# Encoder layer on one core: bias tables built during the first feed-forward, a place for the first value weights, stacks loaded as halves on two queues

## The chip, the cores and the metric

The kernel runs on one core of one Trainium2 chip. A core has a matrix engine (TensorE, PE in the profile; its weight loads are PEld), a vector engine (VectorE, DVE), a scalar engine (ScalarE, ACT), GpSimd (POOL) and a sync engine (SyncE, SP). Here SP and POOL issue nearly all DMAs, that is transfers between the device's memory (DRAM) and the on-chip memory (SBUF). PE writes its results to accumulator banks (PSUM). Each engine works through its own list of instructions in order; a wait of one instruction holds up those behind it on that engine.

The metric is the device time of one execution in microseconds (us). Lower is better.

## The reference, cut to what matters

One layer of a bidirectional encoder, with 1024 tokens of 1024 features, in float32:

```python
h = swiglu(rmsnorm(x, ffn1_pre_g), w_gate, w_up, w_down)      # d_ff = 2816
x = x + 0.5 * rmsnorm(h, ffn1_post_g)
qkv = rmsnorm(x, mix_pre_g) @ w_qkv                           # 16 heads of 64
o_na  = neighbourhood_attention(q[:8], k[:8], v[:8], rel_bias)
o_dil = dilated_mixture_attention(q[8:], k[8:], v[8:], t5_bias)
x = x + rmsnorm(concat(rmsnorm(o_na), rmsnorm(o_dil)) @ w_out, mix_post_g)
x = x + 0.5 * rmsnorm(swiglu(rmsnorm(x, ffn2_pre_g), ...), ffn2_post_g)
```

Neighbourhood (NA) heads attend, on a grid of 16 rows of 64 tokens, to 8 rows by 16 columns around a token, with a learned bias for each head and each offset in rows and columns; what lies outside is masked. Dilated heads mix three windows (128 tokens with step 1, 512 with step 4, 2048 with step 16) under a T5 bias that depends on the distance alone; the three results are weighted by their softmax denominators.

## The kernel before

**Arithmetic.** Each large product in float32 is three matmuls: both operands are split into a high and a low part (`hi`, `lo`: a cast on ACT, then a subtraction on DVE), and hi·hi, hi·lo and lo·hi are summed in a bank (lines 251, 252, 253, called from many places). The large products of the feed-forwards and of q, k and v are made in blocks by a scheme of seven half-size products in place of eight, so sums of operand blocks are made first, and the partial results are kept and combined.

**Stages, by their place in the trace.**

- 0 to 460 us: gate and up products of the first feed-forward, in 22 blocks (`PairGemm`, `NF` = 22). The first nine blocks have two of their seven products done ahead, while the operand is still being made. The rest part runs from about 93 to 460 us with one turn for each block.
- 460 to 683: the down projection (`Passes`: seven passes over the weights, numbered 0 to 6, each with its own weights `pw`, split at lines 602 and 603).
- 683 to 826: the values. Passes 0 and 1 come first (`vp.run(0, 1)`, 683 to 710), then the first products of the query and key blocks (`pg.ahead`, 710 to 765; weights `whi`, `wlo`, lines 344 and 345), then the values' other passes (765 to 826).
- 826 to 938: the rest of the queries and keys, which are written to DRAM (`qk`).
- 938 to 1062: eight dilated heads, two to a pair (`DilPair`). 1062 to 1200: eight NA heads of eight units each (`na_head`, units of 128 queries).
- 1200 to 1350: output projection and norms. 1350 to 1954: the second feed-forward.

**Bias tables.** `build_bias` runs once, during the values. From the T5 bias it makes two tables by a small matmul (`tabp`, line 755), and writes each to DRAM (`tab`) and from there with one DMA of 2 MB (`gab<-tab`, line 760) as 8 heads × 128 shifted rows, so that a head's bias is a plain load later. For the NA heads it fills `nb` in DRAM (8 × 128 × 384) with the mask value (`neg`, line 763), then copies the learned bias into the places that hold it (16 DMAs `nb<-stk`, line 768). All these DMAs are POOL's.

**Attention.** For each head `load_stack` loads the queries and the two halves of the keys (`st`, 128 × 3 × 1024, 1.5 MB) with four DMAs on POOL's queue, two for each half of 64 partitions. The pool `stk` has two places, and `next_head` loads one head ahead. A dilated head needs its bias `g` (two loads on SP, `g<-gab`) and its queries reordered by residue (a copy on POOL, `q`, line 838); an NA head needs `nb` (one load on SP), to which POOL adds the mask (`L1470`, constant `cmask`) for the units at the inside. A unit is: scores (`sp`, lines 933 and 1037), bias, row maximum and exponential on DVE and ACT (lines 849, 851), transposition of the probabilities on PE (`ptp`, line 859) with a copy to SBUF (`pt`, line 861), and the product with the values (`po`, lines 953 and 1053). PE issues scores three units ahead of the transposition and four ahead of the product.

After the second head of a dilated pair `regroup` brings the results of the windows with a step (`ob`) back to token order with 16 DMAs on SP (line 971); `merge` weights them. `na_v` loads a pair's values with 16 DMAs on SP (line 1011).

**Work between the NA units.** When the dilated heads are done, `attended` puts steps on a list (`c.todo`) of which `c.tick()` takes one, four times in an NA head: sums of squares for the norm on ACT (line 1083), scalings on DVE (line 1090), and "puts" (transposition and split of 128 tokens). Then 32 fillers are set up: three matmuls each of the output projection (`accp`, lines 251 to 253), set between the units at the rate `c.rate`; four make one result in the single bank of the pool `psm`, which ACT copies out (line 291).

**What sets the order.** PE's order is the order of the code, and in the first steps and in the attention that of DVE and ACT also. SP and POOL, and DVE and ACT elsewhere, are ordered by a scheduler from the dependencies. `c.behind(f, engines)` gives `f`'s instructions a place after the last instruction so far of those engines; `plan(n, at)` lays steps on the todo list by turn.

## Time and profile before

| | us |
|---|---|
| median of 3 runs | 1958.9 (1957.07 to 1959.87) |
| the profiled execution | 1956.22 |
| its span | 1954.4 |
| TensorE busy | 1867.5 (96% of the span) |
| DVE busy | 1328.8 (68%) |
| ACT busy | 807.7 (41%) |
| POOL busy | 323.8 (17%) |
| data moved by DMA | 398.63 MB, on average 204 GB/s |

A row of the waits reads "engine tile line <- releaser: us in total, times, longest us". The granted clock is the share of full speed that TensorE was given; where it is below 1, the same matmuls take longer. The DMA share is how busy the core's 16 DMA engines were on average. Durations come from the one profiled execution, not from the median of the runs.

### The profile page before, as it was taken

The numbers are of one execution on the slowest core, as the hardware profiler recorded it, in microseconds if no ns is written. First come the engines' busy times: TensorE is split into PE (matmuls) and PEld (weight loads), VectorE is DVE, ScalarE is ACT, GpSimd is POOL, SyncE is SP. The second block draws the span as 40 slices with busy tenths as digits, with TensorE's granted clock in tenths as the row PEclk, the third lists the DMA queues.
The fourth block names the chain that finished last, engine by engine and source line by source line (L and its number), as shares of the span: only waits on it lengthen the run. The fifth ranks groups of instructions, "written<-read, shape, count | busy, mean of one in ns | idle before, by whom it ended". The sixth has DMA issues, their size and how long they took to land.

```text
span 1954.4 us, 25575 instructions
## 1 busy us (share of the span) xinstructions
PE 1867.5 (96%) x9044; PEld 1557.4 (80%) x9044; DVE 1328.8 (68%) x2235; ACT 807.7 (41%) x1463; POOL 323.8 (17%) x520
## 2 busy tenths in 40 slices
PE   5999999999999999999999788998999999999997
PEld 4788888888888778778898777877888888888886
DVE  5778776765656785567576565676788777755567
ACT  4522233333534454133676555454222333345333
POOL 2101111111000123323444220021011111110000
PEclk8999999999999999999999899999999999999999
DMA  6645565546876667868998982475556665476663
GB/s 244 214 169 178 178 236 195 209 165 252 306 255 206 237 242 263 245 195 246 208 190 158 160 147 47 137 264 205 172 177 203 232 229 185 160 255 226 203 226 140
DMA packets 170433, 398.63 MB, mean 204 GB/s; under 512 B 20080, under 2 KB 41504, under 8 KB 170304
## 3 DMA queue, kind: packets, MB, share of 16 engines
q1 hardware_dynamic: 118800, 222.34, 36.2%
q0 software_dynamic: 50640, 172.55, 28.0%
q10 hardware_dynamic: 864, 2.10, 0.3%
q8 instruction: 71, 1.16, 0.3%
q14 instruction: 58, 0.48, 0.1%
HBM read 272.55 MB, written 127.26 MB: 205 GB/s over the span
## 4 chain that ended last, share of the span: by engine, by line
PE 76%; DVE 7%; DMA 7%; issue 5%; ACT 2%; POOL 2%; SPq 1%; DVEq 0%; POOLq 0%; ACTq 0%
PE mmp L253 15%; PE mmp L251 15%; PE mmp L252 14%; PE accp L251 8%; PE accp L252 8%; PE accp L253 8%; PE po L953 2%; DMA wraw<-in_wqk_dram 2%; PE ptp L859 2%; PE trp L159 1%; PE po L1053 1%; DMA st<-qk 1%; PE sp L933 1%; DMA qk<-qk 1%; DVE wlo L345 1%
## 5 line engine op out<-in xcount | busy, mean ns | idle before, releaser
L251 PE MATMUL mmp<-x,whi 128*128 128x512 f32 (+1 forms) x1464 | 581.1, 397 | 8.2 <-ACT whi L344 3.5
L253 PE MATMUL mmp<-x,wlo 128*128 128x512 f32 (+1 forms) x1464 | 576.4, 394 | 1.1 <-DVE wlo L345 1.1
L252 PE MATMUL mmp<-x,whi 128*128 128x512 f32 (+1 forms) x1464 | 575.8, 393 | 0.6 <-DVE x L161 0.5
L251 PEld LDWEIGHTS mmp<-x,whi 128*128 128x128 f32 x1464 | 278.6, 190 | 68.9 <-ACT whi L344 4.2
L253 PEld LDWEIGHTS mmp<-x,wlo 128*128 128x128 f32 x1464 | 278.5, 190 | 62.4 <-DVE wlo L345 1.9
L252 PEld LDWEIGHTS mmp<-x,whi 128*128 128x128 f32 x1464 | 278.8, 190 | 59.7 <-DVE x L161 1.5
L603 DVE TENSOR_TENSOR pw<-praw,pw 128x1024 fp32r<-128x1024 f32 (+1 forms) x182 | 199.2, 1139 | 121.8 <-ACT pw L602 121.6
L602 ACT CAST pw<-praw 128x1024 fp32r<-128x1024 f32 (+1 forms) x182 | 169.0, 982 | 205.6 <-PE accp L253 163.3
L344 ACT CAST whi<-wraw 128x1024 fp32r<-128x1024 f32 x129 | 135.2, 1050 | 249.0 <-PE mmp L252 227.4
L251 PE MATMUL accp<-pw 128*128 128x512 f32 x600 | 234.5, 391 | 0.0
L253 PE MATMUL accp<-pw 128*128 128x512 f32 x600 | 233.8, 390 | 0.0
L252 PE MATMUL accp<-pw 128*128 128x512 f32 x600 | 233.7, 390 | 0.0
L345 DVE TENSOR_TENSOR wlo<-wraw,whi 128x1024 fp32r<-128x1024 f32 x129 | 157.6, 1224 | 24.0 <-ACT whi L344 23.7
L253 PEld LDWEIGHTS accp<-pw 128*128 128x128 f32 x600 | 112.7, 188 | 23.7
L251 PEld LDWEIGHTS accp<-pw 128*128 128x128 f32 x600 | 112.7, 188 | 23.1
L252 PEld LDWEIGHTS accp<-pw 128*128 128x128 f32 x600 | 112.8, 188 | 22.9
L549 POOL DMA_DIRECT2D g<-sg x44 | 23.8, 541 | 473.3 <-DVE sg L542 286.0
L505 DVE TENSOR_TENSOR c<-mmp,u 128x512 f32<-128x512 f32 x52 | 35.9, 691 | 82.9 <-PE mmp L253 82.6
L363 ACT COPY s<-mmp 128x512 f32<-128x512 f32 x52 | 30.5, 586 | 148.8 <-PE mmp L253 147.2
L344 ACT CAST whi<-traw 128x512 fp32r<-128x512 f32 x52 | 32.3, 621 | 117.5 <-DVE traw L433 58.8
L161 DVE TENSOR_TENSOR x<-trp,x 128x512 fp32r<-128x512 f32 x84 | 57.2, 688 | 34.7 <-ACT x L160 34.7
L432 DVE TENSOR_TENSOR wraw<-wraw 128x1024 f32<-128x1024 f32 x52 | 63.6, 1224 | 23.1 <-DMA wraw<-in_wqk_dram 13.5
(229 smaller groups left out, 2781.5 us busy)
## 6 DMA issues: line engine op xcount, KB each, us to landing
praw<-g SPq DMA_DIRECT2D x70, 512.0 KB
wraw<-in_wg_dram SPq DMA_DIRECT2D x44, 512.0 KB
wraw<-in_wu_dram SPq DMA_DIRECT2D x44, 512.0 KB
tr<-in_wd_dram SPq DMA_DIRECT2D x44, 512.0 KB
g<-sg POOLq DMA_DIRECT2D x88, 256.0 KB, 3.7
ts<-tr POOLq DMA_DIRECT2D x22, 1024.0 KB, 4.7
praw<-ts SPq DMA_DIRECT2D x88, 256.0 KB
praw<-in_wd_dram SPq DMA_DIRECT2D x66, 256.0 KB
```

The costliest lines, as they stand in the source:

```text
L161: nc.vector.tensor_sub(lo, ps, hi.bitcast(F32))
L251: nc.tensor.matmul(out, ahi, bhi, start=start, stop=False, skip_group_check=go_on)
L252: nc.tensor.matmul(out, ahi, blo, start=False, stop=False, skip_group_check=go_on)
L253: nc.tensor.matmul(out, alo, bhi, start=False, stop=stop, skip_group_check=go_on)
L344: nc.scalar.copy(hi, raw)
L345: nc.vector.tensor_sub(lo, raw, hi.bitcast(F32))
L432: nc.vector.tensor_sub(r[:, 0:2], r[:, 1:3], r[:, 0:2])
L505: nc.vector.tensor_add(c21, d, u2)
L602: nc.scalar.copy(hi, raw[:, :m])
L603: nc.vector.tensor_sub(lo, raw[:, :m], hi.bitcast(F32))
L859: nc.tensor.transpose(ps[:, j, :], src[:, j * P:(j + 1) * P], c.ident)
L953: nc.tensor.matmul(po[:, un * 2 + j], pt[:, 2 * j + t, :], rhs, start=t == 0, stop=t == 1)
```

## The change

Five things are changed together.

1. **Tables in steps.** `build_bias` becomes `bias_steps`, which gives small steps to 21 of the 22 turns of the first feed-forward's rest part: the copies of the learned bias in turns 1 to 4, loads and the two table matmuls in turns 2 to 5, the shifted rows two heads at a time in turns 4 to 9, clearing in 6 and 7, filling in 8 to 11. In turns 13 to 21 a masked copy of each NA head's table is made (load, addition on POOL, store to the new `nm` in DRAM). Each step goes behind POOL's last instruction. An NA head now loads both `nb` and `nm`, and POOL's addition in the attention is gone.
2. **First value weights.** A pool `p0` of one place holds the split weights of the values' first group, which are fetched before the last steps of the norm are planned; the plan is 12 turns long in place of 8, with the start of the query and key weights at turn 9 and their first split at 11, into the same pool. The pool `pr` has two places in place of three, and the early weights two and `p0`. The first pass always has its first group cut in two.
3. **Stacks.** Of a stack's two halves, one is loaded by POOL's queue and one by SP's. A third place (from the pool `op`) serves every third of the first nine heads, so that a dilated head's stack is loaded two heads ahead.
4. **Regrouping and values.** Eight of the 16 regroupings follow each quad of blocks, where all 16 followed the second; `na_v` has eight DMAs of 16 partitions where it had 16 of eight.
5. **Work between the units.** `attended` now does the first half's squares and scalings, its four puts and the set-up of the fillers, and then the second half's, each with an empty turn between. There are 16 fillers of six matmuls for 32 of three. Two output weights are fetched at the last dilated head.

```diff
-            for k in range(4):
+            for k in (0, 2):
                 def filler(g=g, t=t, k=k, ws=ws, acc=acc):
...
-                    nat_mm(c, acc[0], x, t, k, ws, True, True)
-                    if k == 3:
+                    for i in (k, k + 1):
+                        nat_mm(c, acc[0], x, t, i, ws, True, True)
+                    if k:
                         c.nc.scalar.copy(part[:, t, g * T:(g + 1) * T], acc[0])
...
     def split_left(self, b):
         if b < self.early:
-            self.w[b] = self.split(self.raw.pop(b), "g")
+            self.w[b] = self.split(self.raw.pop(b), "g", self.own if b % 3 == 0 else None)
             self.fetch_left(b + 2)
...
-        if self.own:
-            self.groups[0] = [groups[0][:2], groups[0][2:]] + groups[1:]
+        self.groups[0] = [groups[0][:2], groups[0][2:]] + groups[1:]
...
-def build_bias(c, rel, t5, onehot, lncount):
+def bias_steps(c, rel, t5, onehot, lncount, cmask):
...
+    def step(turn, f, *args):
+        at.setdefault(turn, []).append(lambda: c.behind(lambda: f(*args), POOL))
...
+    def toeplitz(i, h):
         g = c.gab[i]
-        dst = bass.AP(tensor=g.tensor, offset=g.offset, ap=[[P * 640, 8], [641, P], [1, 511]])
-        nc.gpsimd.dma_start(dst, tab[i, :, :511].unsqueeze(1).broadcast_to([8, P, 511]))
+        dst = bass.AP(tensor=g.tensor, offset=g.offset + h * P * 640, ap=[[P * 640, 2], [641, P], [1, 511]])
+        nc.gpsimd.dma_start(dst, tab[i, h:h + 2, :511].unsqueeze(1).broadcast_to([2, P, 511]))
...
+    def masked(h):
+        if h == 0:
+            got["mask"] = c.bp.tile([P, 384], F32, tag="m", name="mask")
+            nc.gpsimd.dma_start(got["mask"], cmask)
+        if h:
+            t = got.pop(h - 1)
+            nc.gpsimd.tensor_add(t, t, got["mask"])
+            nc.gpsimd.dma_start(c.nm[h - 1], t)
+        if h < 8:
+            got[h] = tile("lc" if h % 2 else "oh", 384)
+            nc.gpsimd.dma_start(got[h], c.nb[h].rearrange("p r e -> p (r e)"))
+    for i in range(2):
+        step(2 + 2 * i, load, i)
+        step(3 + 2 * i, table, i)
+        for h in range(4):
+            step(4 + 2 * i + h, toeplitz, i, 2 * h)
+    for cc in range(8):
+        step(1 + cc // 2, stack, cc)
+    step(6, clear, 0)
+    step(7, clear, 4)
+    for r in range(16):
+        step(8 + r // 4, rows, r)
+    for h in range(9):
+        step(13 + h, masked, h)
...
-def load_stack(c, p, hd):
+def load_stack(c, p, hd, pool, bufs):
...
-    for u in range(2):
-        dst = slice(u * 64, u * 64 + 64)
-        nc.gpsimd.dma_start(st[dst, 0, :], q[u, rows, :])
-        nc.gpsimd.dma_start(st[dst, 1:3, :], k[:, rows, :].rearrange("j p n -> p j n"))
+    for u, queue in enumerate((nc.gpsimd, nc.sync)):
+        to = st[u * 64:u * 64 + 64].bitcast(F32)
+        queue.dma_start(to[:, 0, :], q[u, rows, :])
+        queue.dma_start(to[:, 1:3, :], k[:, rows, :].rearrange("j p n -> p j n"))
...
-        if (hd, part, quad) == (1, 1, 1):
-            self.regroup()
+        if hd and part:
+            self.regroup(quad)
...
-    for r in range(16):
-        c.nc.sync.dma_start(vs[r * 8:r * 8 + 8], src[r])
+    for ci in range(8):
+        c.nc.sync.dma_start(vs[ci:P:8], src[ci])
...
     c.nc.sync.dma_start(nb[:, 0], c.nb[2 * p + hd].rearrange("p r e -> p (r e)"))
+    c.nc.sync.dma_start(nb[:, 1], c.nm[2 * p + hd])
...
-            c.pr, c.pw, c.vt = pool("pr", 3, e), pool("pw", 2, e), pool("vt", 2, e)
+            c.pr, c.pw, c.vt = pool("pr", 2, e), pool("pw", 2, e), pool("vt", 2, e)
...
-            plan(8, {0: [lambda: fin.scale(4, 4), A(4, 5)], 4: [U(4)], 5: [lambda: queued(pg.start)]})
+            p0 = pg.own = pool("p0", 1, prep, side="right")
+            vp.fetch([[p0.tile([P, 2, T], F32R, tag="g" + h, name="pw0" + h) for h in ("hi", "lo")]])
+            plan(12, {0: [lambda: fin.scale(4, 4), A(4, 5)], 8: [U(4)], 9: [lambda: queued(pg.start)],
+                      11: [lambda: pg.split_left(0)]})
...
-            build_bias(c, a["na_rel_bias"], a["t5_rel_bias"], a["onehot"], a["lncount"])
...
-            c.todo.extend([lambda: (queued(c.w.fetch), squares[0]()), squares[1], scales[0],
-                           lambda: (scales[1](), queued(c.w.fetch))]
-                          + puts[:4] + [begin] + puts[4:])
+            c.todo.extend([squares[0], scales[0]] + puts[:4] + [begin, squares[1], lambda: None, scales[1]])
+            for f in puts[4:]:
+                c.todo.extend([lambda: None, f])
...
+            i = next(stacked, None)
+            if i is not None:
+                own = i < 9 and i % 3 == 2
+                stacks.append(load_stack(c, *heads[i], c.op if own else c.stk, 1 if own else 2))
...
-                    else:
-                        nc.gpsimd.tensor_add(g[:, 1], g[:, 0], c.cmask)
...
+                    if (p, hd) == (2 * NP - 1, 1):
+                        queued(lambda: [c.w.fetch() for _ in range(2)])
```

**ACT at the first value weights.** In the list of ACT before, from the last copies of the down projection's stage to the first value copy (`x_…` are operand tiles of the values, `junk,fss` the sums of squares of the norm, `vt` a value result copied out of its bank):

```order
L160 CAST x_4765<-trp 128x4x128
L151 ACTIVATE junk,fss<-hb 128x512
L160 CAST x_4767<-trp 128x4x128
L151 ACTIVATE junk,fss<-hb 128x512 x2
L602 CAST pw<-praw 128x1024
L151 ACTIVATE junk,fss<-hb 128x512
L602 CAST pw<-praw 128x1024
L1362 COPY vt<-accp 128x512
```

After:

```order
L603 CAST pw0hi<-praw 128x1024
L160 CAST x_4858<-trp 128x4x128
L160 CAST x_4860<-trp 128x4x128
L160 CAST x_4858<-trp 128x4x128
L151 ACTIVATE junk,fss<-hb 128x512
L160 CAST x_4860<-trp 128x4x128
L151 ACTIVATE junk,fss<-hb 128x512 x2
L603 CAST pw<-praw 128x1024
L151 ACTIVATE junk,fss<-hb 128x512
L603 CAST pw<-praw 128x1024
L1427 COPY vt<-accp 128x512
L345 CAST whi<-graw 128x1024
```

The first group's cast (`pw0hi`) has moved ahead of the last operand tiles, and the query and key weights' first cast (`whi`) stands right behind the first value copy; before it came some 15 rows later.

**SP from the last dilated heads to the first NA heads**, before (`vs` are an NA pair's values; `g`, `nb` and `obn` as above):

```order
L971 DMA obn<-ob 32x2x132 x16
L895 DMA g<-gab_68 128x384
L895 DMA g<-gab_69 128x384
L1011 DMA vs<-v_87 8x8x128 x17
L1017 DMA nb<-nb 128x384
L971 DMA obn<-ob 32x2x132 x16
L1017 DMA nb<-nb 128x384
L1011 DMA vs<-v_87 8x8x128 x15
```

After:

```order
L1057 DMA vs<-v_87 16x8x128 x8
L1063 DMA nb<-nb 128x384
L1064 DMA nb<-nm 128x384
L106 DMA wraw<-in_wo_dram 128x1024 x2
L1017 DMA obn<-ob 32x2x132 x16
L876 DMA st<-qk_0_73 64x1024
L877 DMA st<-qk_1_74 64x2x1024
L1063 DMA nb<-nb 128x384
L1064 DMA nb<-nm 128x384
L1057 DMA vs<-v_87 16x8x128 x8
```

The last 16 regroupings have moved behind the output weights (`wraw`) and ahead of a stack's half (`st`), which SP did not issue before; each head's `nb` load is followed by one of `nm`.

**PE at the first fillers**, between NA units (`o_…` is the dilated heads' normed result, `accp` the bank of the output projection), before:

```order
L859 MATMUL ptp<-ident,pb 128x128 x3
L251 MATMUL accp<-whi,o_9559 128x512
L252 MATMUL accp<-wlo,o_9559 128x512
L253 MATMUL accp<-whi,o_9559 128x512
L1053 MATMUL po<-vs,pt 128x128 x2
L1037 MATMUL sp<-st 128x384 x2
```

After:

```order
L904 MATMUL ptp<-ident,pb 128x128 x2
L251 MATMUL accp<-whi,o_9591 128x512
L252 MATMUL accp<-wlo,o_9591 128x512
L253 MATMUL accp<-whi,o_9591 128x512
L251 MATMUL accp<-whi,o_9591 128x512
L252 MATMUL accp<-wlo,o_9591 128x512
L253 MATMUL accp<-whi,o_9591 128x512
L1100 MATMUL po<-vs,pt 128x128 x2
L1084 MATMUL sp<-st 128x384 x2
```

Fillers come six matmuls at a time, in every second unit; before, three came in nearly every unit.

More of the change, by code (lines that the diff above doesn't have):

```diff
@@ L592, in fetch @@
             w = c.pr.tile([P, 1 + self.own, 2, 2, T], F32R, tag="w", name="pw")
-            w = [w[:, side] for side in range(1 + self.own)]
+            w = [[w[:, side, h] for h in range(2)] for side in range(1 + self.own)]
         for side in range(1 + self.own):
@@ L600, in fetch @@
                     nc.sync.dma_start(raw[:, j], self.right(i)[b])
-            hi, lo = [w[side][:, h, :m] for h in range(2)]
+            hi, lo = [x[:, :m] for x in w[side]]
             nc.scalar.copy(hi, raw[:, :m])
@@ L604, in fetch @@
         for j, i in enumerate(ids):
[L605 to L606 removed]
+            lhs = [x[:, j, :] for x in w[0]] if self.own else [h[:, i, :] for h in self.left.x[a]]
+            self.ready.append((lhs, [x[:, j, :] for x in w[-1]]))
     def run(self, *which, upto=6):
@@ L1169, in plan @@
             c.todo.extend(turn(at.get(i, ())) for i in range(n))
-        def one_a_turn(steps, n, first):
-            plan(n, {first + i: [f] for i, f in enumerate(steps)})
         def spread(steps, n, skip=0):
@@ L1191, in gate_pairs, with ffn @@
             return PairGemm(c, op, [(wg[f], wu[f]) for f in range(NF)], early, GatePairs(c, which))
-        def ffn(which, op, prep, pg, get, turns, sums, more, post, pre, src, dst, begin=None):
+        def ffn(which, op, prep, pg, get, turns, sums, more, post, pre, src, dst, begin=None, tables={}):
             w = sub()
@@ L1217, in ffn @@
             pg.begin_rest()
-            one_a_turn(sums, NF, NF - 3 - len(sums))
+            tables = {k: list(f) for k, f in tables.items()}
+            if tables:
+                c.bp = pool("bp", 1, w)
+            for i, f in enumerate(sums):
+                tables.setdefault(NF - 3 - len(sums) + i, []).append(f)
+            plan(NF, tables)
             prep2, ps = sub(), []
```

99 lines of the change are left out of this document (54 added, 45 removed).

## The prediction

> **What bounds the kernel now.** I read the page's first two parts first, then busy time by stage, then TensorE's waits in the stages where it isn't full.
>
> ```profile
> PE 1867.5 (96%) x9044; PEld 1557.4 (80%) x9044; DVE 1328.8 (68%) x2235; ACT 807.7 (41%) x1463; POOL 323.8 (17%) x520
> PEclk8999999999999999999999899999999999999999
> ```
>
> TensorE (PE) is busy 96% of the span, so the change, which takes no matmul away, can win only where PE stands still or runs at a lowered clock. The stages (columns: stretch, length, busy us of PE, PE's weight loads, DVE, ACT and POOL, then the granted clock, the DMA share and GB/s):
>
> ```profile
> 60.00:660.00 600.00, 598.94 (x2659) 492.94 (x2658) 427.90 (x539) 223.93 (x305) 65.22 (x115) 1.00 0.62 218
> 660.00:720.00 60.00, 54.66 (x252) 42.87 (x251) 42.16 (x81) 27.43 (x47) 11.88 (x22) 1.00 0.63 223
> 780.00:860.00 80.00, 76.09 (x323) 60.68 (x322) 46.91 (x60) 18.81 (x22) 25.47 (x42) 0.98 0.72 224
> 960.00:1060.00 100.00, 95.50 (x838) 94.39 (x836) 66.40 (x276) 73.18 (x253) 41.03 (x42) 1.00 0.95 176
> 1060.00:1100.00 40.00, 32.74 (x223) 30.35 (x222) 19.45 (x69) 16.88 (x52) 15.46 (x19) 0.87 0.93 161
> 1100.00:1140.00 40.00, 28.90 (x194) 25.78 (x193) 30.07 (x93) 26.08 (x85) 7.24 (x11) 0.91 0.89 153
> 1140.00:1200.00 60.00, 57.40 (x379) 52.00 (x380) 30.80 (x92) 34.48 (x91) 6.50 (x10) 0.97 0.58 110
> ```
>
> The 600 us of the feed-forward are full (598.94 busy). The change touches the other rows, the largest lost shares in 1060 to 1140: idle 7.3 and 11.1 us, and the clock (0.87 and 0.91 of 40 us) loses about 5.2 and 3.6 us more. The DMA engines are nearly full there (0.93, 0.89), the fact that speaks most against a gain.
>
> **A: a place for the first value weights (660 to 720).** PE's waits there:
>
> ```profile
> PE accp L252 <- DVE pw L603: 2.0, 3, 1.0
> PE mmp L251 <- ACT whi L344: 1.7, 1, 1.7
> PE accp L251 <- ACT pw L602: 0.8, 1, 0.8
> ```
>
> They are 4.5 of the 60 − 54.7 = 5.3 us that PE stands: it waits for the first value weights and for the first weights of the queries and keys to be split into high and low parts. Now the first are fetched while the down projection still runs, and the second are split before the values end (pool p0 holds both in turn). I take 4.0 off, because the split merely moves into a stretch where ACT and DVE have room (27.4 and 42.2 of 60). Bounds: 5.3 off, or 1 lost, if the split of QK's weights holds up a value copy behind it on ACT for the longest of these waits less what it saves.
>
> **B: the tables leave the values stage (780 to 860).** PE loses 3.9 us and 2% of clock (1.6). POOL's queue there waits for two tables of 2 MB to land (the last two rows: the landings of all loads and stores of nb, and the tables' issues, with KB and us to landing), at a DMA share of 0.72, against 0.62 in the feed-forward:
>
> ```profile
> POOL nb L768 <- DMA gab<-tab: 16.3, 2, 14.8
> ...
> DVE u L470 <- DMA s<-s1d: 2.9, 1, 2.9
> ...
> PE mmp L251 <- DVE c L497: 2.0, 1, 2.0
> ...
> PE accp L252 <- DVE pw L603: 1.9, 1, 1.9
> ```
>
> ```profile
> DMA to landing us min/median/max: 2.1/4.1/20.2
> ```
>
> ```profile
> gab<-tab POOLq DMA_DIRECT2D x2, 2044.0 KB, 20.5
> ```
>
> DVE made its operand (c) late because the sum s1d, read back from memory, came 2.9 us late. With the two tables, the cleared and the filled bias (1.5 MB each) gone, some 7 MB, such loads come earlier. I take 4.0 off of 5.5; bounds 0 (pr has one place less and this stage's weights may be late anyhow) and 5.5.
>
> **C: the way into the neighbourhood heads (1060 to 1100).** The chain of waits, with columns start, length, what, and PE's waits and SP's queue in the same stretch:
>
> ```profile
> 1063.24 10.28 DMA obn<-ob
> ...
> 1077.51 2.94 DMA nb<-nb
> ...
> 1080.70 0.09 POOL nb L1470
> ...
> 1083.23 11.40 DMA st<-qk
> ...
> 1094.76 0.48 PE sp L1037 x2
> ```
>
> ```profile
> PE po L1053 <- DVE pt L861: 3.2, 1, 3.2
> PE sp L1037 <- DMA st<-qk: 2.1, 1, 2.1
> ```
>
> ```profile
> 1046.61 14.65 SPq L1011 DMA_DIRECT2D vs<-v  x17
> 1061.91 15.49 SPq L971 DMA_DIRECT2D obn<-ob  x16
> ```
>
> Sixteen regroupings (15.5 us of SP) stand ahead of a bias load; POOL's mask addition waits for that load, and the next stack, issued by POOL behind the addition, takes 11.4 us more while PE starves. The change cuts three links: half of the regroupings go out a quad earlier and eight value loads replace 16 (half of 14.65 us), the addition is gone (a masked table is loaded), and a third place lets a stack start one dilated head sooner, some 15 us (eight heads from 938 to 1062). That should remove 3.2 + 2.1 us of waits and 5.2 us of clock; I keep 2 back for the second bias load (1.5 MB in all) and the two output weights (1 MB) that now come in at this point: 8.5 off. Bounds 0 and 10.5.
>
> **D: order of the norm and the fillers (1100 to 1220).**
>
> ```profile
> PE ptp L859 <- DVE pt L861: 4.5, 2, 3.0
> PE po L1053 <- ACT pt L861: 3.0, 1, 3.0
> PE sp L1037 <- DVE stt L849: 1.7, 1, 1.7
> ...
> PE accp L251 <- ACT hs L291: 3.4, 4, 1.0
> ```
>
> ```profile
> L1083 ACT ACTIVATE junk<-og 128x256 bf16<-128x256 f32 x16 | 6.4, 402 | 0.0
> L1083 ACT ACTIVATION_READ_ACCUMULATOR junk<-og 128x1 f32 x16 | 3.0, 189 | 0.0
> L1090 DVE SCALAR_TENSOR_TENSOR og<-og,y,gd 128x512 f32<-128x512 f32 x8 | 6.2, 838 | 0.0
> ```
>
> Here 9.4 us of squares on ACT and 6.2 of scalings on DVE come in lumps between the softmax steps, and the transposed probabilities (pt) queue behind them: 9.2 us of PE waits in the first three rows and 3.6 of clock. After the change one half's squares and scalings are followed by four puts and the first fillers, and the other half comes later, so a lump is half as long and PE has filler matmuls sooner. I take 6 of 12.8: half the waits, and the clock's part with them. Bounds 0 and 11. The fourth row (1140 to 1220) is four waits for the one accumulator bank, each where the next filler stood right behind the last of a bank. Six matmuls in every second unit put a whole unit between: 3.0 off, bounds 1 lost and 3.4.
>
> **E: what is added.** The tables now go to POOL's queue in 21 turns of the feed-forward's 60–460 us, where PE is full and DMA is at 0.62: about 7 MB as before, and 3 MB to read a table, add the mask and write it back, some 10 MB over 360 us or 28 GB/s on 218. Its 8 additions cost POOL, by the next row, 8 × 1.0 to 1.2 us:
>
> ```profile
> L1470 POOL TENSOR_TENSOR nb<-nb,cmask 128x384 f32<-128x384 f32 x3 | 3.6, 1203 | 1.0 <-DVE y L144 1.0
> ```
>
> The work is hidden by POOL's idleness (65 of 600 busy). Behind each waiting table step stand the stores of gate products, which nobody loads before the down projection; if that cover is gone, DVE waits for a place to write, then PE. Two table matmuls stay as they were. SP gets two stack issues and one bias issue more per head, 3 × 0.53 = 1.6 us (the bias load's issue in the queue's rows was 0.35 to 0.53), less the eight value issues. I take 1.7 lost for all of it; bounds 0 and 8 (half of the 16.3 us of POOL waits above, passed on).
>
> **The stacks' halves** go out on two queues. Loads of 64 partitions on POOL's queue, against POOL's loads and stores of all 128 in the feed-forward (200 to 400):
>
> ```profile
> st<-qk POOLq DMA_DIRECT2D x4, 512.0 KB, 8.7
> q0 software_dynamic: 896, 3.15, 47.6%
> ...
> q0 software_dynamic: 5600, 19.93, 25.8%
> ```
>
> A packet took 0.476 × 40 us × 16 / 896 = 340 ns in halves (1140 to 1180) and 147 ns in the feed-forward, at the same 3.5 KB. Half the partitions seem to use about half of what lies on the way; two halves side by side would then land a stack in little over half the time. Of C's 8.5 us I put 3 on this. The Trainium skill disagrees with itself: "DMA: Bandwidth & Descriptors", section "Rules for kernel authors", says of two transfers to disjoint partition halves that they serialize and aren't worth it; "SBUF — State Buffer", section "Door 1: The DMA port swizzle (why `[64,N]` ≈ `[32,N]`)", says that 64 neighbouring partitions reach only half of the 16 ports. No run here shows two halves side by side; the packets favour the second. By the first, the sum would be 3 us smaller.
>
> **Sum.** Among the dilated heads PE waits once for POOL's copy of a late stack, which two heads of lead should end:
>
> ```profile
> PE sp L933 <- POOL q L838: 0.8, 1, 0.8
> ```
>
> −4.0 − 4.0 − 8.5 − 6.0 − 3.0 − 0.8 + 1.7 = −24.6. The profiled execution took 1956.22 us (span 1954.4), 2.7 below the median of 1958.9. So 1931.6 in its terms and 1934 against the median. A change under 0.2% (3.9 us) can't be told from none here.
>
> **Rivals.**
>
> *Attention stays paced by DMA.* For: shares of 0.95, 0.93 and 0.89; the change sends no byte less through these heads, but 1.5 MB more. Against: 0.58 in the last of them, with PE full. Then only A, B and the fillers pay: −4 − 4 − 3 = −11, 1948 us.
>
> *The table steps hold up the feed-forward (slower).* POOL's queue waits there for landings (4.1 us median, 16.3 for the big tables) with gate stores behind each. Passed on in full, 16.3 + 8 × 4.1 = 49 us come to PE; less the 25 won elsewhere, 1983. It decides from the point where the stalls of a turn exceed the stores' slack, and nets zero at 25 us passed on. Against: 535 idle us of POOL in that row.
>
> *SP's queue now waits for a stack's place (slower).* In the neighbourhood heads POOL waits for the place before it issues:
>
> ```profile
> POOL st L831 <- PE sp L1037: 63.3, 5, 16.8
> ```
>
> That is 1090 to 1210; nothing else stood behind it. Now SP waits the same time, with bias and value loads of the next head behind it. If the bias is late by as much as the longest of the PE waits in C, 3.2 us a head over seven heads, that is +22 against the −11 of the first rival: 1970. It decides once a place comes free later than one load before its head begins; the order of SP puts the stack ahead of the same head's bias, which is what speaks for it.
>
> *The halves gain nothing.* Two transfers side by side share what one has: C keeps 3 us, 1937, inside my own range.
>
> **Chances.** My sum 0.60 (0.20 of it with halves that gain nothing), paced by DMA 0.18, tables 0.10, SP's queue 0.12. My sum's own range is 1922 (A to D near their ends, −36) to 1945 (half of C and D missing). For 8 in 10, the low end is 1918 and the high end reaches over the DMA case and the near part of SP's to 1962. Faster is 0.60 + 0.16 of the DMA case; the other 0.02 of it and 0.03 of the two slow cases lie within 0.2%; slower is the remaining 0.19.
>
> **What would show it.** A and B: PE's waits for pw, whi and c gone in those stretches, and the granted clock of B at 1.00. C: no chain through obn, nb and st, no mask addition, a 512 KB half landing nearer 5 than 8.7 us. D: the 4.5 and 3.0 us rows halved, the bank's four waits gone. E: PE still 599 of 600 in the feed-forward; any drop there, or PE waits for bias tiles in the neighbourhood heads, makes me wrong. So does a clock that stays below 0.95 from 1060 to 1140.

## The result and the profile after

The changed kernel takes 1982.7 us (median of four runs, 1980.95 to 1988.07) where the kernel before took 1959.4 beside it: a ratio of 1.0121, with a 95% interval of 1.0107 to 1.0136. It is 23 us slower; 25 us faster were forecast.

The first two parts of the page of the changed kernel (busy time; granted clock in 40 slices):

```profile
PE 1874.5 (95%) x9044; PEld 1562.2 (79%) x9044; DVE 1326.4 (67%) x2235; ACT 808.0 (41%) x1463; POOL 322.4 (16%) x513
PEclk8998898999999999999999989999999999999999
```

PE has the same 9044 matmuls, but the clock now dips in slices 4, 5 and 7, from about 150 to 250 and from 300 to 350 us, where it had been full before. Where the stages begin shows how the time is shared out. By the first matmul of each stage in the two traces:

| from the first matmul of … | before | after | difference |
|---|---|---|---|
| start to the down projection (gate and up products) | 469.0 | 518.8 | +49.8 |
| down projection, first values | 244.0 | 241.2 | −2.8 |
| first products of queries and keys | 52.1 | 51.1 | −1.0 |
| values, rest | 58.7 | 56.7 | −2.0 |
| queries and keys, rest | 114.1 | 109.1 | −5.0 |
| dilated heads | 123.4 | 126.9 | +3.5 |
| NA heads to the second feed-forward | 228.3 | 211.0 | −17.3 |
| second feed-forward, to the last matmul | 653.9 | 655.0 | +1.1 |

Between the gate and up products and the second feed-forward the change wins 24.6 us, close to the 26.3 of the forecast without its last term. The loss is in the first stage, but for 1.1 us of the second feed-forward, which the change doesn't touch. Stretches of the first stage, of the kernel before and then of the changed one (columns as in the prediction):

```profile
160.00:260.00 100.00, 100.00 (x438) 82.11 (x437) 78.82 (x102) 27.97 (x37) 14.17 (x25) 1.00 0.56 197
260.00:420.00 160.00, 160.00 (x698) 131.06 (x697) 115.81 (x140) 55.17 (x76) 21.21 (x36) 1.00 0.59 213
```

```profile
160.00:260.00 100.00, 79.09 (x317) 62.27 (x316) 56.59 (x75) 18.91 (x23) 20.69 (x31) 0.86 0.53 171
260.00:420.00 160.00, 147.59 (x618) 118.48 (x617) 102.72 (x129) 48.19 (x67) 38.45 (x63) 0.96 0.61 210
```

PE stands for 33 of these 260 us; most of the other 17 that the stage lost go with the lowered clock (0.86 and 0.96). The DMA share does not rise; in the worst stretch it even falls, from 0.56 to 0.53, and less is moved (171 for 197 GB/s) although table traffic has been added. Something slow is not something busy. What PE and DVE wait for (changed kernel, 100 to 460 us):

```profile
PE mmp L251 <- DVE c L499: 22.3, 4, 10.9
DVE wraw L434 <- DMA wraw<-in_wu_dram: 15.8, 6, 8.0
...
PE tabp L766 <- DMA oh<-in_onehot_dram: 8.8, 1, 8.8
```

The longest of PE's four waits for DVE, 10.9 us, comes from weights: DVE waits for `wu`, makes its operand (`c`) late, and PE waits for that. (Two others, 6.5 and 4.2 us, come from 308 us on and are taken up under the second rival below.) Once PE itself stands before the table's small matmul. The chain of waits from 160 to 240 us has both:

```profile
168.03 1.12 POOL gab L773
169.15 0.59 POOL tt L759
169.75 16.30 DMA oh<-in_onehot_dram
186.04 0.14 issue
186.18 1.86 PE tabp L766 x2
...
216.17 12.80 DMA wraw<-in_wu_dram
...
232.94 0.61 DVE c L499
233.55 0.04 issue
233.59 0.80 PE mmp L251
```

A load of 64 KB took 16.3 us. It was issued right behind `gab<-tab`, the shifted rows of two heads. The landings in this stretch (160 to 260 us; KB each, median us from issue to landing) name the slow transfer:

```profile
gab<-tab POOLq DMA_DIRECT2D x6, 511.0 KB, 17.0
wraw<-in_wg_dram SPq DMA_DIRECT2D x5, 512.0 KB, 10.0
wraw<-in_wu_dram SPq DMA_DIRECT2D x5, 512.0 KB, 12.7
```

511 KB of shifted rows take 17.0 us. Before the change two DMAs of 2044 KB each, side by side and over eight heads, landed in 20.5: eight times the bytes in hardly more time. In the trace's packet records the first of the new DMAs is 84 packets of 6132 bytes, of which one or two run at once for 13.0 of 13.3 us and never more than three; the two of before have 16 or 17 packets at once for 12.4 of their 20 us, and about eight at their start and end, when one of them runs alone. Packets of 12 bytes stand beside the large ones: 4704 for 672 in the whole changed kernel, which is 14 for each two, and 672 for 672 before, which is eight for each eight; 16 in all both times. At 9 ns each they take little time. The records don't name the engine, but by both counts a DMA with two heads outermost runs on two of the 16 DMA engines, and one with eight heads on eight. A weight load that is spread over all 16 is complete only when its packets on those two are, too. That was the theory with which the experiments began.

The packet records show this wait directly. Two weight loads were issued at 171.4 and 172.0 us and landed at 181.4 and 184.7, while the first rows DMA ran. The mean number of packets in flight:

| stretch of the changed kernel, us | weights | shifted rows | all |
|---|---|---|---|
| 174.0 to 175.5 | 14.5 | 2.0 | 16.6 |
| 176.5 to 185.0 | 0.6 | 1.4 | 2.1 |

Most of the weights' packets were through by 176.5 us. For the 8.5 us behind that about two packets ran at a time, rows and the last of the weights in turn, so most of the 16 engines stood idle. With the tables back in the values (the first experiment below) the same two loads had 16.5 packets in flight at their height and landed after 3.9 and 4.7 us.

### The profile page after: what moved, and what is told of

It reads as the page before. It is cut to its first block, busy times and chain, and to the rows that moved or that the text cites. A ratio compares the mean times of both kernels' runs of the same rounds, so it can differ in the third digit from the quotient of the medians.

```text
span 1980.8 us, 25583 instructions
## 1 busy us (share of the span) xinstructions
PE 1874.5 (95%) x9044; PEld 1562.2 (79%) x9044; DVE 1326.4 (67%) x2235; ACT 808.0 (41%) x1463; POOL 322.4 (16%) x513
## 4 chain that ended last, share of the span: by engine, by line
PE 76%; DMA 11%; DVE 7%; ACT 2%; issue 2%; SPq 1%; POOL 0%; DVEq 0%; ACTq 0%; POOLq 0%
PE mmp L251 15%; PE mmp L252 15%; PE mmp L253 15%; PE accp L252 8%; PE accp L253 8%; PE accp L251 8%; DMA tr<-in_wd_dram 2%; PE po L998 2%; DMA wraw<-in_wu_dram 2%; PE trp L159 2%; PE ptp L904 2%; PE po L1100 1%; PE sp L978 1%; DMA ts<-tr 1%; DMA oh<-in_onehot_dram 1%
## 5 line engine op out<-in xcount | busy, mean ns | idle before, releaser
L251 PE MATMUL mmp<-x,whi 128*128 128x512 f32 (+1 forms) x1464 | 584.9, 400 | 28.4 <-DVE c L499 22.3
```

The source lines that it names most:

```text
L251: nc.tensor.matmul(out, ahi, bhi, start=start, stop=False, skip_group_check=go_on)
```

## The experiments

Each kernel's runs stand beside runs of the kernel before on the same chip. On the chip of experiments 1 to 4 the kernel before took 1963.6 us, on those of 5 to 8 and 9 to 12 it took 1959.6 and 1959.0; a comparison across chips is therefore given by the ratios on 1959 us, and by the medians where these say something else. Times of stages are from one profiled execution of each kernel. "Tables back" below is the first experiment, and several others start from it.

**1. The tables go back.** Only the first part of the change is undone:

```diff
-    bias_steps(c, *[a[k] for k in ("na_rel_bias", "t5_rel_bias", "onehot", "lncount", "cmask")]))
+    )
...
             pg.fetch(1)
+            build_bias(c, a["na_rel_bias"], a["t5_rel_bias"], a["onehot"], a["lncount"])
             vp.run(4, 5)
...
-    c.nc.sync.dma_start(nb[:, 1], c.nm[2 * p + hd])
...
+                    else:
+                        nc.gpsimd.tensor_add(g[:, 1], g[:, 0], c.cmask)
```

> Everything of the change but its first part: the tables are built in one go during the values and the mask is added in the attention, as before. If the table steps alone cost the 50 us that the first feed-forward is longer, the down projection starts near 469 us again and the time is about 1959 - 22 = 1937 us. If the other parts had a hand in it (pools, a longer plan, stacks on SP), it stays above 1960.

Measured 1937.4 us, ratio 0.9856 (0.9828 to 0.9884); the down projection starts at 469.6 us. The table steps cost all of the loss, and the other four parts win 1.4%, as expected.

**2. The tables alone**, put into the kernel before.

```diff
+    bias_steps(c, *[a[k] for k in ("na_rel_bias", "t5_rel_bias", "onehot", "lncount", "cmask")]))
...
-            build_bias(c, a["na_rel_bias"], a["t5_rel_bias"], a["onehot"], a["lncount"])
...
+    c.nc.sync.dma_start(nb[:, 1], c.nm[2 * p + hd])
...
-                    else:
-                        nc.gpsimd.tensor_add(g[:, 1], g[:, 0], c.cmask)
```

> The kernel before with only the first part of the change: table steps in the feed-forward, masked tables loaded in the attention. If the table steps cost 50 us by themselves: 1959 + 50, less some 5 us that the values win without tables, about 2004 us. If they cost only together with the other parts: 1955 to 1965.

Measured 1998.9 us, ratio 1.0182 (1.0159 to 1.0204), that is +36 us by the ratio, where about 45 were expected. The down projection starts at 519.4 us, as in the changed kernel: the 50 us come with the table steps alone. By the medians about 14 come back later. The profile, of the slowest of the four executions (2003.6 us), shows about half of that: 5.2 us in the rest of the queries and keys and 2.3 from the NA heads on, with 4.7 lost again in the dilated heads and the second feed-forward.

**3. Rows outermost.** The same bytes, instructions and places; only the order in which a DMA walks them differs:

```diff
-        dst = bass.AP(tensor=g.tensor, offset=g.offset + h * P * 640, ap=[[P * 640, 2], [641, P], [1, 511]])
-        nc.gpsimd.dma_start(dst, tab[i, h:h + 2, :511].unsqueeze(1).broadcast_to([2, P, 511]))
+        dst = bass.AP(tensor=g.tensor, offset=g.offset + h * P * 640, ap=[[641, P], [P * 640, 2], [1, 511]])
+        nc.gpsimd.dma_start(dst, tab[i, h:h + 2, :511].unsqueeze(0).broadcast_to([P, 2, 511]))
```

> The changed kernel, but each DMA of two heads of shifted rows walks the 128 rows outermost and the heads inside; same bytes, same instructions, same places. Theory 'two engines': as changed, one such DMA runs one or two packets at a time for 13 us, on two of the 16 DMA engines, and every weight load that is spread over all engines waits for those two; with 128 outermost it is spread over all, lands in 4 to 6 us, and most of the stalls from 186 to 260 us go: 1945 to 1960 us. Theory 'order and volume': the steps cost by their place in POOL's queue and their 10 MB, whatever the shape: within 5 us of 1982.

**4. Eight heads in a DMA**, so that eight is the outermost size:

```diff
-        dst = bass.AP(tensor=g.tensor, offset=g.offset + h * P * 640, ap=[[P * 640, 2], [641, P], [1, 511]])
-        nc.gpsimd.dma_start(dst, tab[i, h:h + 2, :511].unsqueeze(1).broadcast_to([2, P, 511]))
+        dst = bass.AP(tensor=g.tensor, offset=g.offset + h * P * 640, ap=[[P * 640, 8], [641, P], [1, 511]])
+        nc.gpsimd.dma_start(dst, tab[i, h:h + 8, :511].unsqueeze(1).broadcast_to([8, P, 511]))
...
-        for h in range(4):
-            step(4 + 2 * i + h, toeplitz, i, 2 * h)
+        step(4 + 2 * i, toeplitz, i, 0)
```

> The changed kernel, but the shifted rows of a table go out as one DMA of 2 MB over eight heads (as before the change), in the turns of the first of the four. 'Two engines': eight engines share what two had, so a stall is shorter but the queue is full for 20 us: between the changed kernel and the one with rows outermost, 1955 to 1975. 'Order and volume': within 5 us of 1982.

Rows outermost: 1946.2 us, ratio 0.9912 (0.9890 to 0.9935). Eight heads: 1965.0, ratio 1.0016 (0.9997 to 1.0034). With two, eight and 128 as the outermost size the kernel is 1.2% slower than before, the same, and 0.9% faster; the down projection starts at 518.8, 496.8 and 481.4 us (469.0 before). Both medians lie in the ranges that were expected under "two engines". Landings from 160 to 260 us with the tables back, with rows outermost, and with eight heads:

```profile
wraw<-in_wg_dram SPq DMA_DIRECT2D x6, 512.0 KB, 4.1
wraw<-in_wu_dram SPq DMA_DIRECT2D x6, 512.0 KB, 5.8
```

```profile
gab<-tab POOLq DMA_DIRECT2D x8, 511.0 KB, 7.3
wraw<-in_wg_dram SPq DMA_DIRECT2D x6, 512.0 KB, 6.6
wraw<-in_wu_dram SPq DMA_DIRECT2D x6, 512.0 KB, 7.7
...
oh<-in_onehot_dram POOLq DMA_DIRECT2D x1, 63.9 KB, 6.0
```

```profile
gab<-tab POOLq DMA_DIRECT2D x2, 2044.0 KB, 17.9
wraw<-in_wg_dram SPq DMA_DIRECT2D x5, 512.0 KB, 6.2
wraw<-in_wu_dram SPq DMA_DIRECT2D x5, 512.0 KB, 8.3
```

The rows land in 7.3 us for 17.0, the weights in 6.6 and 7.7 for 10.0 and 12.7, and the small load in 6.0 for 16.3, so that PE no longer waits at the table's matmul. With eight heads that wait stays, since the load stands behind 2 MB on the same queue (17.6 us to land). That the volume or the place in POOL's queue alone costs the 50 us falls: with rows outermost neither was altered, and 37 of the 50 went. (With eight heads the rows also go out in fewer DMAs and turns, so that step says less by itself.) The Trainium skill states the mechanism in "DMA: Bandwidth & Descriptors", section "Rules for kernel authors": the slowest dimension of a DMA's access pattern sets how many engines it uses, so an outermost size below 16 confines it to at most that many. The landings agree with it, and so do the packets that run at once: one or two with two heads, up to eight for nearly all of the time with eight, up to 16 with 128 rows, where the first copy's large packets are through in 3.5 us and packets of 12 bytes are absent.

Rows outermost still had one stall, of 5.6 us up to 222.8: two DMAs of rows and a clearing of 0.75 MB had been issued from 199.2 to 202.2 us, and the next weight load, issued at 202.5, took 11.0.

**5. Spread steps**: rows outermost, and one DMA of rows in a turn, clearing in four pieces (from a tile of its own), filling earlier and two rows of the grid in a turn.

```diff
...
-            step(4 + 2 * i + h, toeplitz, i, 2 * h)
+            step(4 + 4 * i + h, toeplitz, i, 2 * h)
...
-    step(6, clear, 0)
-    step(7, clear, 4)
+    for h in range(4):
+        step(h, clear, 2 * h)
...
-        step(8 + r // 4, rows, r)
+        step(5 + r // 2, rows, r)
```

> Rows outermost, and besides one DMA of shifted rows a turn (turns 4 to 11 for 4 to 9, where two turns had two), clearing in four pieces in turns 0 to 3, filling two rows of the grid a turn. With rows outermost alone PE still lost about 9 us at 222 us, after two row DMAs and a clearing of 0.75 MB had been issued in one turn and the next weight load took 11 us. If that bunch is the rest of the loss, the down projection starts near 470 us (481 with rows outermost alone) and the time is about 1937 us; if the 10 MB cost by themselves, it stays at 1944 to 1948.

**6. Spread, and no masked tables**: POOL adds the mask in the attention.

```diff
-    for h in range(9):
-        step(13 + h, masked, h)
...
-    c.nc.sync.dma_start(nb[:, 1], c.nm[2 * p + hd])
...
+                    else:
+                        nc.gpsimd.tensor_add(g[:, 1], g[:, 0], c.cmask)
```

> The same, but no masked tables: POOL adds the mask in the attention as before, and an NA head loads one bias table. Attention to the end of the output projection took 340 us with masked tables and rows outermost, 332 us with the tables left in the values. If the second bias load (1.5 MB over the eight NA heads) is that difference: 5 to 8 us below the run before it, about 1931 us. If it is chance of the order: within 3 us.

Spread: 1939.2 us, ratio 0.9890 (0.9868 to 0.9911). Without masked tables: 1934.3, ratio 0.9864 (0.9845 to 0.9884). The stretch that had stalled, with rows outermost and then with the steps spread:

```profile
160.00:260.00 100.00, 94.39 (x398) 75.72 (x397) 71.64 (x95) 25.86 (x33) 28.05 (x48) 0.97 0.70 224
```

```profile
160.00:260.00 100.00, 99.19 (x431) 80.19 (x430) 78.89 (x104) 28.64 (x36) 28.66 (x49) 1.00 0.73 237
```

So the bunch was most of what was left: at a share of 0.73 PE is full, at 0.53 with two engines blocked it was not. The down projection starts at 474 us with spread steps and at 473 without masked tables, not quite at 469. Which of the moves (rows, clearing, filling) did it was not parted. The masked tables cost 5 us more by the medians, which is what was expected; in the profiles the stretch from the NA heads to the second feed-forward takes 208.1 us with them and 203.2 without. With them PE waits once for about 5 us at a filler, while ACT waits for an output weight. That wait stands in each of the four profiles with masked tables and the new fillers, and in none that has the new fillers without masked tables. How the tables make the weight late was not tried. The rows are those of the spread kernel, 1065 to 1274 us:

```profile
PE accp L251 <- ACT hs L292: 5.2, 1, 5.2
...
ACT whi L116 <- DMA wraw<-in_wo_dram: 3.8, 1, 3.8
```

**7. Both halves on one queue**, from "tables back":

```diff
-    for u, queue in enumerate((nc.gpsimd, nc.sync)):
+    for u, queue in enumerate((nc.gpsimd, nc.gpsimd)):
```

> As with the tables back in the values (1937), but both halves of a stack on POOL's queue, four DMAs, two places and a third as changed. If two halves side by side land sooner and that is worth 3 us, as the prediction put it: about 1940. If they serialize: 1937. If SP's queue loses by them, since bias loads of the dilated heads stand behind a stack's half (DVE waited 16.3 us for them, 1.7 before the change): 1932 to 1935.

Measured 1942.4 us, ratio 0.9915 (0.9893 to 0.9937): 5 us slower than "tables back" by the medians and 12 by the ratios. Two queues pay. The time is near the 1940 that was expected if halves land sooner, but that is not why: no half lands in half the time. In the changed kernel, from 1130 to 1230 us, a half of the keys took 9.1 and 8.0 us, and 8.7 in the kernel of this experiment with both on one queue (1090 to 1190):

```profile
st<-qk POOLq DMA_DIRECT2D x5, 512.0 KB, 9.1
st<-qk SPq DMA_DIRECT2D x4, 512.0 KB, 8.0
```

```profile
st<-qk POOLq DMA_DIRECT2D x10, 512.0 KB, 8.7
```

With the tables back, from which this experiment starts, it is 9.8 us on POOL's queue and 7.2 on SP's (1085 to 1185). On this the runs agree with the rule of the Trainium skill that the prediction cites, that two halves serialize. Where the 5 to 12 us come from stays open. In the profiles they lie among the dilated heads, which took 139.7 us with one queue and 129.0 with two. There the bias loads landed later (8.5 us for 5.0 with the tables back), and PE waited 15.8 us for the probabilities `pt` in place of 6.2; but DVE's own waits for the bias were shorter (10.0 us for 16.3), and nothing was tried to part the causes.

**8. The bias first**, from "tables back":

```diff
-            if i != 9:
-                load_st()
-            if i:
-                load_rest()
+            if 0 < i < 9:
+                load_rest()
+            if i != 9:
+                load_st()
+            if i > 8:
+                load_rest()
```

> As with the tables back in the values, but among the dilated heads the next head's bias is asked for ahead of the stack of the head after it. If the bias loads are late because they stand behind a stack's half on SP, the dilated heads fall from 129 us to 124 and the time to about 1933; if they are late because the DMA engines are full (share 0.9), no change.

Measured 1925.0 us, ratio 0.9822 (0.9804 to 0.9839): 12 us below "tables back" by the medians, 7 by the ratios, more than the 4 expected. The dilated heads took 120.4 us for 129.0. The rows of the bias loads among the dilated heads, with the tables back and with the bias first:

```profile
DVE s L925 <- DMA g<-gab: 16.3, 5, 5.4
```

```profile
g<-gab SPq DMA_DIRECT2D x12, 192.0 KB, 5.0
```

```profile
g<-gab SPq DMA_DIRECT2D x12, 192.0 KB, 2.7
```

DVE's 16.3 us of waits are absent with the bias first, and PE's wait for `pt` on ACT's side (6.2 us there) with them. It was the order on SP, not the full DMA engines, that made the bias late.

**9. Both gains together**: experiment 6 with the edit of experiment 8.

```diff
+            if 0 < i < 9:
+                load_rest()
             if i != 9:
                 load_st()
-            if i:
+            if i > 8:
                 load_rest()
```

> What won so far together: table steps in the feed-forward, spread, rows outermost, no masked tables, and the bias asked for ahead of the stack among the dilated heads. If the two gains add up (3 us of the spread steps without masked tables against the tables in the values, 12 of the bias first): about 1922 us. If the bias order pays only with the tables in the values: about 1934.

Measured 1926.7 us (1919.9 to 1929.5), ratio 0.9835 (0.9807 to 0.9862). About 1922 was expected. It can't be told from experiment 8, so the table steps win nothing measurable on top. By the ratios there was nothing to add: 0.9864 without masked tables, 0.9856 with the tables back. Experiments 9 and 8 beat the kernel before by 1.7% and 1.8%.

**10 to 12. Three other parts undone one by one**, each from "tables back".

The first weights (10):

```diff
...
-            p0 = pg.own = pool("p0", 1, prep, side="right")
-            vp.fetch([[p0.tile([P, 2, T], F32R, tag="g" + h, name="pw0" + h) for h in ("hi", "lo")]])
-            plan(12, {0: [lambda: fin.scale(4, 4), A(4, 5)], 8: [U(4)], 9: [lambda: queued(pg.start)],
-                      11: [lambda: pg.split_left(0)]})
+            plan(8, {0: [lambda: fin.scale(4, 4), A(4, 5)], 4: [U(4)], 5: [lambda: queued(pg.start)]})
```

> As with the tables back in the values (1937), and also without the place for the first value weights, the longer plan and the early split of the query and key weights. The prediction put 4.0 us on it: 1941. If the stage is limited by something else: 1937, within 2.

The order of the norm, and 32 fillers (11; the fillers' lines as in the diff of the change):

```diff
-            c.todo.extend([squares[0], scales[0]] + puts[:4] + [begin, squares[1], lambda: None, scales[1]])
-            for f in puts[4:]:
-                c.todo.extend([lambda: None, f])
+            c.todo.extend([squares[0], squares[1], scales[0], scales[1]] + puts[:4] + [begin] + puts[4:])
```

> As with the tables back in the values (1937), but with the old order of squares, scalings and puts and with 32 fillers of three matmuls. The prediction put 6 + 3 us on the new ones: 1946. If the stack loads carry the attention's gain: 1937 to 1940.

The third place (12):

```diff
-                own = i < 9 and i % 3 == 2
+                own = False
...
-            if i != 9:
-                load_st()
-            if i:
-                load_rest()
+            if i != 1:
+                load_head()
```

> As with the tables back in the values (1937), but with two places for stacks and each loaded one head ahead, as before; halves still on two queues. The prediction put 8.5 us on the way into the neighbourhood heads, 3 of them on the halves (measured 5 by the run with one queue). If the third place carries the rest: 1941 to 1943. If the halves alone do: 1937. If the lead only makes bias loads late on SP, as the run with the bias first suggests: 1930 to 1934.

| part undone | median, us | ratio (95%) | above "tables back": by medians, by ratios |
|---|---|---|---|
| 10: first weights | 1938.3 | 0.9890 (0.9868 to 0.9913) | 1, 7 |
| 11: norm order and fillers | 1946.2 | 0.9936 (0.9908 to 0.9963) | 9, 16 |
| 12: third place | 1939.4 | 0.9894 (0.9871 to 0.9918) | 2, 7 |

"Tables back" ran on the chip on which the kernel before was 4.6 us slower, hence the two figures; no run says which of the two is nearer. Only experiment 11 is clear of the noise: the intervals of 10 and 12 overlap that of "tables back" (0.9828 to 0.9884). For the first weights the profiles say more than the totals: the down projection with the first values takes 245.2 us for 241.8, and the next stage 52.1 for 51.1, in all 4.4 us where 4.0 were expected. For the third place they say no more: the dilated heads take 127.5 us for 129.0 and what follows them 206.7 for 203.4. With the old order and fillers that stretch takes 215.6. In the traces the waits come back. Without the first weights, 660 to 725 us, the rows are those of before:

```profile
PE accp L252 <- DVE pw L605: 2.0, 3, 1.0
PE mmp L251 <- ACT whi L345: 1.7, 1, 1.7
...
PE accp L251 <- ACT pw L604: 0.8, 1, 0.8
```

With the old order and fillers, 1064 to 1210 us (4.5 and 3.4 us before):

```profile
PE ptp L934 <- DVE pt L936: 4.8, 2, 2.5
...
PE accp L251 <- ACT hs L291: 3.4, 4, 1.0
```

## Why the prediction was wrong

**What bounds the kernel.** Right: PE at 96%, and waits as the only thing to win. The gains came mostly where the waits were read.

**A.** Forecast −4.0. The changed kernel's down projection and first values gained 2.8 us and the next stage 1.0; undoing it alone cost 4.4 us in these two stages. Right, and the three rows of waits came back when it was undone. Of the waits for `pw`, which were to be gone, 1.7 us stayed in the changed kernel.

**B.** Forecast −4.0. The rest of the values gained 2.0 and that of the queries and keys 5.0 in the changed kernel. With the tables back in this very stage, these two took 59.6 and 113.2 us, almost as before (58.7 and 114.1), so the table traffic was the cause, as put. A little more than forecast, and most of it a stage later: the queries and keys took 108.8 to 110.4 us in all seven profiles with table steps and 111.4 to 114.2 in all seven without. PE's wait for `c` is gone, as forecast; the one for `pw` (1.9 us before, 2.0 after) is not.

**C and D.** Forecast −8.5, −6.0, −3.0 and −0.8, in all −18.3; the dilated and NA heads and what follows gained 13.8 in the changed kernel. In the first 40 us of the NA heads, where C put its gain, PE is busy for 35.1 us at a clock of 0.99, where it was 32.7 at 0.87. D as a whole is shown (9 to 16 us, where 9 were forecast), though order and fillers were not parted, and in the changed kernel one wait of 5.2 us at a filler took the place of the four of 3.4. In C the halves did not land faster, the step that failed there, and yet two queues were worth 5 to 12 us for a reason that stays open. The two places of the Trainium skill that the prediction set against each other speak of different things, two transfers side by side and the ports that one transfer reaches, and the 340 ns of a packet did not decide for two side by side. That the third place pays is not shown. And the third rival happened on a small scale, in another place than it was put: not in the NA heads but among the dilated ones, bias loads stood behind a stack's half on SP; the order of the two was worth 7 to 12 us.

**E is the step that failed.** It was put at +1.7 us with a bound of 8; it was +49.8. The term said that the work was hidden because POOL was idle and 10 MB over 360 us are 28 GB/s. Both are true, and both are means. What counted most was the shape of each DMA: the change had cut one DMA over eight heads into four over two, and with that moved it to two engines at a time. The prediction costed the edit by bytes and never by engines. Before the change two DMAs over eight heads ran side by side and so had all 16 engines between them; a row of landings alone (20.5 us for 2044 KB) did not show what one over two heads would do, but the access pattern in the diff, with the packets that ran at once, would have. The term also said that the two table matmuls "stay as they were"; on PE they now stood in a full stage, and PE waited 8.8 us for the load of one, with the clock lowered in that stretch. The term named one path to PE itself, the gate stores, and bounded it at 8 us.

**The second rival** gave 1983 us, and 1982.7 was measured. That number is luck: its price, 49 us, was made from POOL's waits for the two big tables and from median landings of `nb`, none of them in the feed-forward, passed on to PE in full. Its mechanism, POOL's queue holding gate stores until DVE waits for a place to write, happened in part. DVE has such waits in the changed kernel and had none before (100 to 460 us):

```profile
DVE sg L528 <- DMA g<-sg: 6.4, 2, 4.8
DVE c L499 <- DMA g<-c: 5.9, 1, 5.9
```

PE's waits of 6.5 us up to 314 and of 4.2 us up to 361 come behind these, and behind late loads for the sums of the down weights (`tr`). Its others, 8.8, 1.2 and 10.9 us, come behind the loads of a table and of weights, with no wait for a gate store in the chain. So the rival has part of about a third of PE's 32 us of waits. Rows outermost left each step where it was in POOL's queue and took 37 of the 50 us away, with most of both kinds of wait; as it also lets POOL's own landings come sooner, that run doesn't part the two paths, and only the chains do. The chance of 0.10 was too low because the only thing weighed against it was POOL's idleness.

**The chances** put 0.76 on faster. Without part E the sum would have been −26.3 us, or −22.3 without B also, which goes when the tables are back in the values; that kernel is 1.44% or 28 us faster than before. So the rest of the sum was not too high, and the forecast failed by one term of seven.

## What to carry to other kernels

Cost a DMA by its shape as well as by its bytes: here an outermost size of two put it on two DMA engines, and transfers that were spread over all of them waited for these two, although the mean DMA share stayed low. So compare landing times for each size of transfer, not the share alone; and when a large DMA is cut into small steps, cut it so that the outermost size stays large, and don't bunch them in one turn beside loads that have little slack. When a queue gets a new kind of load, ask which of its loads is needed first, and issue that one first.

## What the runs showed of the hardware that had not been expected

- Weight loads of 512 KB, spread over all DMA engines, took 10.0 and 12.7 us while another DMA occupied one or two engines at a time, against 4.1 and 5.8 without it, at a mean DMA share of 0.53 and 0.56.
- While such a DMA ran, two weight loads had 14.5 packets in flight beside its 2.0, and then for 8.5 us about two packets ran in all, 1.4 of the copy and 0.6 of the weights.
- DRAM-to-DRAM copies of the same table rows with outermost sizes of 2, 8 and 128: 511 KB in 17.0 us, 2044 KB in 17.9, 511 KB in 7.3.
- A load of 64 KB issued on the same queue right behind such a copy landed after 16.3 us (two outermost), 17.6 (eight) and 6.0 (128).
- In the NA heads two halves of 64 partitions on two queues landed hardly sooner than on one queue (9.1 and 8.0, or 9.8 and 7.2, against 8.7 us), and the kernel was 5 to 12 us faster with two queues all the same.
